# The second mixer of a two-layer trunk put as a whole into a region of fixed instruction order

## The chip, the cores and the metric

The kernel runs on one core of a Trainium2 chip. The metric is the device time of one execution in microseconds (us); lower is better. In the kernel before, three timed runs gave a median of 1370.22 us.

## The reference

512 tokens of width 1024 pass through two layers, with 16 learned tokens put in front (528 columns in all). Layer 0 is a sparse attention and layer 1 a differential attention over a shared key and value set; after each stands a gated feed-forward block with a short convolution. The part that matters here is layer 1's mixer:

```python
kv = rms_norm(h, kv_norm_g) @ w_kv_b
k1, k2, vb = jnp.split(kv, [...], axis=-1)
k1 = rms_norm(k1.reshape(B, Tp, N_HEADS, B_HEAD_DIM), kn_b)
k2 = rms_norm(k2.reshape(B, Tp, N_HEADS, B_HEAD_DIM), kn_b)
...
def attn_map(qb, kk):
    lg = jnp.einsum('bqhd,bshd->bhqs', qb, kk).astype(jnp.float32) * scale + bias
    return jax.nn.softmax(jnp.where(mask, lg, NEG_INF), axis=-1)
a = attn_map(q1b, k1) - lam * attn_map(q2b, k2)
o = jnp.einsum('bhqs,bshd->bqhd', a.astype(vb.dtype), vb)
...
o = rms_norm(o, sub_g) * (1.0 - lam_init)
return o.reshape(B, Tp, N_HEADS * B_V_DIM) @ w_o
```

## The kernel before

**Data.** The residual stream `ht` lies in SBUF as eight tiles of 128 features by 528 tokens. Every projection is float32 made of three matmuls: a weight is cast to a short float32 by ScalarE (`hi`, L168), the remainder is taken by VectorE or GpSimd (`lo`, L176), the activations are split alike (`xh`, `xl`), and TensorE (`lin`, L306) adds hi·hi, hi·lo and lo·hi. A weight's way is a DMA on SyncE (L115), a scaling by the norm's gains on GpSimd (`raw`, L123), then `hi` and `lo`; three buffers of each kind rotate, and the work for the unit three ahead is written into the source where a unit ends (`done`, which calls `pump`).

**The second mixer** (`mixer_b`, L1471) starts with the norm of the first 272 columns, still missing from `ffn(0)`, then takes four pairs of heads p = 0 to 3. `project(p)` (L1500) makes two key, two query and two value projections of 48 matmuls each. When one ends, ScalarE and VectorE take it out of PSUM: keys as squares `sq` and scaled `kg` (L1513, L1514), queries as `qst` twice and `sq` (L1529 to L1532), values as `vf` (L1571). TensorE then sums squares (`stk` L671, `stq` L681), the reciprocal roots are made on ScalarE and VectorE (`rsqrt`, L470 to L478), GpSimd spreads a key's root (`ex`, L698) and TensorE turns it (`Rk`, L703); values are turned too (`vt`, L713).

`attend_b` (L1605) runs 16 units, two heads by two halves of the queries per pair. A unit scores the next unit's blocks (`sb`, L1670 and L1671; VectorE adds the bias and takes the minimum, L1673; ScalarE takes the exponential, L1679; VectorE combines the two maps, L1689 to L1692) while it multiplies its own with the values, in steps: a transpose `pt` (L1759), `ph` by ScalarE (L1763), `pl` by VectorE (L1764), and three matmuls `pv` (L1745); at its end ScalarE copies `of` (L1767). Between the pieces `fill` (L274) takes matmuls of the projections from a generator, 6 at a time as a rule, until a model clock of the source has gone on by the gap that the pair asks for (`GAP_B`). A generator may hand back nothing: query projections of a pair wait until attention has come to a certain unit. `defer` writes a piece into the source once the model clock has passed a delay. `finish_sums` (L1780) writes the squares of the outputs (`sqo`, L1788) and, straight behind them, their sum on TensorE (`stq`); `finish_roots`, `Ro` (L1819) and `split_out` finish a pair's outputs, and `wo_first` and `wo_last` multiply them with the output weights.

```python
def sums(e):
    sq = bp.tile([128, T], F32, tag="sq", name="sqo", bufs=2)
    nc.scalar.activation(sq[:, t0:t1], of[:, e, t0:t1], AF.Square)
    st = self.query_stats(sq, self.ones, blocks)
```

**What sets the order.** The program is built with `schedule_with_timeline_sim=True`: a scheduler plays the instructions through on a model of the engines and issues, on each engine, what is ready, the earlier in the source first. `high_priority` lets the norm's pieces go ahead by 200 places. In `ffn` the 20 paired blocks stand in `tc.manual_schedule(engines=ENGINES)`, where TensorE, VectorE and ScalarE (`ENGINES`) keep the source's order; GpSimd and SyncE are always left to the scheduler. There the casts are placed by hand (`early`, `late`, with `auto = False`); in `mixer_b` they stand where `done` calls `pump`. PSUM has two tiles of two banks (tag `sp`: `lin`, `Rk`, `vt`) and four of one bank (tag `one`: `sb`, `pt`, `pv`, the sums).

Of the kernel before, what the change touches and what calls it, by code (L numbers as in the profile page):

```python
# [15 lines left out]
ENGINES = {mybir.EngineType.PE, mybir.EngineType.DVE, mybir.EngineType.Activation}  # L16
# [1860 lines left out]
@with_exitstack  # L1877
def trunk_kernel(ctx, tc, aps, out):
    t = Trunk(ctx, tc, aps, out)
    t.setup()  # L1880
    t.mixer_a()
    t.ffn(0)
    t.mixer_b()
    t.ffn(1)


# [53 lines left out]
```

## Time and profile before

| | |
|---|---|
| median of 3 runs | 1370.22 us (1365.03 to 1372.44) |
| the profiled execution | 1369.62 us, span 1367.8 us |
| TensorE matmul busy | 1284.9 us, 94% of the span |
| VectorE busy | 1032.4 us, 75% |
| ScalarE busy | 716.7 us, 52% |
| GpSimd busy | 343.3 us, 25% |
| mean granted TensorE clock | 0.975 of full speed |

Busy time of TensorE holds the time in which a matmul is under way, pipelined ones included, so the distance from start to start is shorter than a row's mean duration. An engine's "idle before" is the time before an instruction in which the engine did nothing, with the releaser that ended it. A granted clock of 1.00 is 2.4 GHz, 0.50 is 1.2 GHz, and a value between is a mean over a stretch that had both. The second mixer lies between about 655 and 985 us of the span.

### The profile page before, as it was taken

What the parts mean: (1) busy time and instruction counts of PE and PEld (TensorE: products, weight loads), DVE (VectorE), ACT (ScalarE), POOL (GpSimd) and SP (SyncE); (2) the same over time, 40 slices, a digit from 0 to 9 for tenths busy, and PEclk for the clock granted to TensorE, in tenths of its full rate; (3) what the DMA queues carried; (4) which work ended last, traced back from release to release, by engine and by line L of the source; (5) the groups of instructions that cost most, each with busy time, mean ns of one, the idle gap of its engine ahead of it and who ended that gap; (6) DMA issues with size and microseconds to landing.
All of it is one profiled execution on the core that took longest, in us unless ns stands there. A gap on an engine that the chain in (4) does not pass through costs nothing.

```text
span 1367.8 us, 25126 instructions
## 1 busy us (share of the span) xinstructions
PE 1284.9 (94%) x9688; PEld 1233.5 (90%) x9688; DVE 1032.4 (75%) x2030; ACT 716.7 (52%) x1426; POOL 343.3 (25%) x398
## 2 busy tenths in 40 slices
PE   5999889897999999989899999989897999999998
PEld 4999889897999999989799999989787999999986
DVE  6499977687888888776657777776787888888873
ACT  4453555564555555554435555655464555555541
POOL 3513543410111111103444644444510111111100
PEclk9999999989999999999899989999999999999999
DMA  7312222121455445533222222212221454554432
GB/s 236 107 61 76 88 83 80 62 78 62 117 133 146 127 125 130 132 79 106 92 63 89 68 67 63 71 48 73 67 88 62 120 146 129 127 148 127 118 90 93
DMA packets 58519, 136.03 MB, mean 99 GB/s; under 512 B 7216, under 2 KB 16736, under 8 KB 58400
## 3 DMA queue, kind: packets, MB, share of 16 engines
q1 hardware_dynamic: 48432, 114.57, 25.7%
q0 software_dynamic: 9968, 19.87, 9.5%
q8 instruction: 76, 1.25, 0.4%
q14 instruction: 43, 0.35, 0.1%
HBM read 112.46 MB, written 4.91 MB: 86 GB/s over the span
## 4 chain that ended last, share of the span: by engine, by line
PE 80%; DVE 11%; ACT 4%; issue 2%; POOL 1%; DMA 1%; SPq 0%; ACTq 0%; DVEq 0%; POOLq 0%
PE lin L306 22%; PE dn L1374 18%; PE g L1240 17%; PE v L1240 12%; DVE c L1331 2%; PE pv L1745 1%; PE stq L681 1%; PE pv L1119 1%; PE linh L306 1%; DVE lo L176 1%; DVE xl L630 1%; ACT hi L168 1%; PE sa L1024 1%; PE stk L671 1%; PE sb L1671 1%
## 5 line engine op out<-in xcount | busy, mean ns | idle before, releaser
L306 PE MATMUL lin<-xh,hi 128*128 128x256 f32 (+3 forms) x928 | 272.2, 298 | 13.6 <-DVE ht L547 7.1
L306 PE MATMUL lin<-xl,hi 128*128 128x256 f32 (+3 forms) x928 | 272.3, 295 | 2.1 <-DVE xl L630 1.8
L306 PE MATMUL lin<-xh,lo 128*128 128x256 f32 (+3 forms) x928 | 271.8, 294 | 0.0
L168 ACT CAST hi<-raw 128x512 fp32r<-128x512 f32 (+3 forms) x225 | 178.8, 824 | 90.9 <-PE lin L306 47.6
L176 DVE TENSOR_TENSOR lo<-raw,hi 128x1024 fp32r<-128x1024 f32 (+3 forms) x196 | 179.1, 929 | 55.1 <-ACT hi L168 52.1
L1410 POOL DMA_DIRECT2D ht<-y x64 | 55.8, 872 | 569.3 <-ACT y L1409 560.6
L306 PEld LDWEIGHTS lin<-xh,hi 128*128 128x128 f32 (+1 forms) x928 | 179.7, 196 | 17.1 <-ACT xh L656 8.6
L306 PEld LDWEIGHTS lin<-xl,hi 128*128 128x128 f32 (+1 forms) x928 | 181.2, 195 | 3.8 <-DVE xl L630 3.2
L306 PEld LDWEIGHTS lin<-xh,lo 128*128 128x128 f32 (+1 forms) x928 | 181.1, 195 | 0.0
L1240 PE MATMUL g<-xh,hi 128*128 128x264 f32 (+1 forms) x480 | 137.3, 286 | 11.3 <-DVE c L1331 6.6
L1374 PE MATMUL dn<-al,hi 128*128 128x256 f32 (+2 forms) x528 | 143.0, 321 | 0.0
L1374 PE MATMUL dn<-ah,lo 128*128 128x256 f32 (+2 forms) x528 | 142.2, 320 | 0.0
L1374 PE MATMUL dn<-ah,hi 128*128 128x256 f32 (+2 forms) x528 | 142.2, 321 | 0.0
L1240 PE MATMUL v<-Th,lo 128*128 128x264 f32 (+1 forms) x480 | 136.9, 285 | 0.0
L1240 PE MATMUL v<-Tl,hi 128*128 128x264 f32 (+1 forms) x480 | 136.5, 284 | 0.0
L1240 PE MATMUL v<-Th,hi 128*128 128x264 f32 (+1 forms) x480 | 136.3, 284 | 0.0
L1240 PE MATMUL g<-xh,lo 128*128 128x264 f32 (+1 forms) x480 | 136.0, 283 | 0.0
L1240 PE MATMUL g<-xl,hi 128*128 128x264 f32 (+1 forms) x480 | 135.7, 283 | 0.0
L1240 PEld LDWEIGHTS g<-xh,hi 128*128 128x128 f32 x480 | 90.4, 188 | 15.4 <-ACT hi L168 7.7
L176 DVE TENSOR_TENSOR lo<-S,hi 128x1024 fp32r<-128x1024 f32 x80 | 97.2, 1216 | 0.0
L1374 PEld LDWEIGHTS dn<-ah,lo 128*128 128x128 f32 x528 | 89.0, 188 | 7.4
L1374 PEld LDWEIGHTS dn<-ah,hi 128*128 128x128 f32 x528 | 88.8, 188 | 5.7 <-ACT hi L168 1.1
(301 smaller groups left out, 3290.7 us busy)
## 6 DMA issues: line engine op xcount, KB each, us to landing
raw<-w_up SPq DMA_DIRECT2D x88, 512.0 KB, 3.7
raw<-w_down SPq DMA_DIRECT2D x64, 256.0 KB, 3.5
ht<-y POOLq DMA_DIRECT2D x32, 264.0 KB, 3.9
raw<-w_in SPq DMA_DIRECT2D x16, 512.0 KB, 3.6
raw<-w_kv SPq DMA_DIRECT2D x16, 512.0 KB, 3.6
ht<-y POOLq DMA_DIRECT2D x32, 256.0 KB, 3.8
raw<-w_down SPq DMA_DIRECT2D x16, 384.0 KB, 3.2
nb<-nbias SPq DMA_DIRECT2D x16, 264.0 KB, 2.7
```

The costliest lines, as they stand in the source:

```text
L168: nc.scalar.copy(hi[:, :n, :m], src)
L176: eng.tensor_tensor(lt[:, :n, :m], src, hi[:, :n, :m].bitcast(F32), op=OP.subtract)
L306: i = self.nc.tensor.matmul(o, w[wi][:, kw + k, :m], x[s][xi][:, kx + k, c0:HN[s]], start=(first and p == 0), stop=(last and p == 2))
L630: i = eng.tensor_tensor(xl[:, m, o:o + n], xfs[m][:, :n], xh[:, m, o:o + n].bitcast(F32), op=OP.subtract)
L671: self.nc.tensor.matmul(st[:88, 2 * c:2 * c + 2], sq[:, 88 * c:88 * (c + 1)], rhs, start=True, stop=True)
L681: self.nc.tensor.matmul(st[:, c:c + 2], sq[:, c0:c0 + 128], rhs, start=True, stop=True)
L1024: nc.tensor.matmul(s, q[:, c0:c0 + 128], k[:, k0:k1], start=(p == 0), stop=(p == 2))
L1119: nc.tensor.matmul(pv[:, :4 * nq], v[:, c, :], pp[:, :, :nq], start=(ci == 0 and p == 0), stop=(ci == nch - 1 and p == 2))
L1240: nc.tensor.matmul(out, w[wi][:, wk + k, :], xs[xi][:, xk + k, c0:c0 + N], start=(first and k == 0 and p == 0), stop=(k == 3 and p == 2), ...
L1331: nc.vector.scalar_tensor_tensor(t[:, z:n], u[:, off + t0 + z - d:off + T - d], w, t[:, z:n], op0=OP.mult, op1=OP.add)
L1374: nc.tensor.matmul(part(t, c0, c1, o), w[wi][:, k, :], acts[f][ai][:, c0:c1], start=(first and p == 0), stop=(last and p == 2))
L1410: nc.gpsimd.dma_start(self.h[m][:, t0:T], y[:, :n], accum_op=OP.add)
```

## The change

The call of `mixer_b` is put into the region that `ffn` already uses. The statements in it and their order in the source stay as they are.

```diff
     t.setup()
     t.mixer_a()
     t.ffn(0)
-    t.mixer_b()
+    with tc.manual_schedule(engines=ENGINES):
+        t.mixer_b()
     t.ffn(1)
```

Of the orders of TensorE, VectorE and ScalarE, all rows of the second mixer may move. Three places follow; the attention of the second pair of heads runs in each of them, beside the projections of the third.

ScalarE, where `finish_sums` for the first pair is written, behind the second key projection. Before:

```order
L1679 ACTIVATE xs,ss<-xs,sm 128x272
L1679 ACTIVATE xs,sm<-xs,sm 128x272
L168 CAST hi<-raw 128x1024
L1529 ACTIVATE qst<-lin,gs 64x528
L1767 COPY of<-pv 128x272
L1788 ACTIVATE sqo<-of 128x528
L1763 CAST ph<-pt 128x256
```

With the change:

```order
L1763 CAST ph<-pt 128x256 x3
L1513 ACTIVATE sq<-lin 128x528
L1514 ACTIVATE kg<-lin,par 128x528
L168 CAST hi<-raw 128x1024
L1788 ACTIVATE sqo<-of 128x528 x2
L1763 CAST ph<-pt 128x128
```

The squares `sqo` stood by themselves between pieces of attention, and now stand behind the evacuation of a key projection and a weight cast. On TensorE, in the change, the sum `stq<-ones,sqo` follows `pt` with no matmul between.

VectorE, where the first key projection of the third pair ends. Before:

```order
L1692 SCALAR_TENSOR_TENSOR xx<-xx,sm 128x400
L1764 TENSOR_TENSOR pl<-pt,ph 128x128
L1673 ISA xs,sm<-sb,tm,rq 128x272
L1673 ISA sm 128x1
L1673 ISA xs,sm<-sb,tm,rq 128x272
L1673 ISA sm 128x1
L1689 RECIPROCAL sm<-sm 128x1
L1690 SCALAR_TENSOR_TENSOR sm<-ss,nlam,sm 128x1
L1692 SCALAR_TENSOR_TENSOR xs<-xs,sm 128x272
L176 TENSOR_TENSOR lo<-raw,hi 128x1024
```

With the change:

```order
L1692 SCALAR_TENSOR_TENSOR xx<-xx,sm 128x528
L176 TENSOR_TENSOR lo<-raw,hi 128x1024
L1689 RECIPROCAL sm<-sm 128x1
L1690 SCALAR_TENSOR_TENSOR sm<-ss,nlam,sm 128x1
L1692 SCALAR_TENSOR_TENSOR xx<-xx,sm 128x400
L1673 ISA xs,sm<-sb,tm,rq 128x272
L1673 ISA sm 128x1
L1673 ISA xs,sm<-sb,tm,rq 128x272
L1673 ISA sm 128x1
L1519 TENSOR_SCALAR rk<-stk 88x12
L1764 TENSOR_TENSOR pl<-pt,ph 128x256
```

The weight's remainder `lo` moved ahead of a combination and of two score reductions, which stand in the queue behind it now.

TensorE, where the first query projection of the third pair has ended and the generator of projections hands back nothing. Before, a piece of the same unit:

```order
L306 MATMUL lin<-xh_8145,hi 128x272
L306 MATMUL lin<-xl_8146,hi 128x272
L1745 MATMUL pv<-pl,vh 128x256
L1745 MATMUL pv<-ph,vl 128x256
L1759 MATMUL pt<-ident,xx 128x128 x2
L306 MATMUL lin<-xh_8145,lo 128x272
L306 MATMUL lin<-xh_7979,hi 128x256
L306 MATMUL lin<-xl_7980,hi 128x256
L1670 MATMUL sb<-kst,qst 128x16
L1671 MATMUL sb<-kl_8073,qst 128x16
L306 MATMUL lin<-xh_7979,lo 128x256
```

With the change, 12 rows out of a run of 25 instructions without a `lin`:

```order
L1745 MATMUL pv<-ph,vl 128x272
L1759 MATMUL pt<-ident,xs 128x128 x2
L1670 MATMUL sb<-kst,qst 128x400
L1671 MATMUL sb<-kl_8071,qst 128x400
L1670 MATMUL sb<-kst,qst 128x400
L1671 MATMUL sb<-kl_8079,qst 128x400
L681 MATMUL stq<-ind,sq 128x2 x5
L1745 MATMUL pv<-ph,vh 128x256
L1745 MATMUL pv<-pl,vh 128x256
L1745 MATMUL pv<-ph,vl 128x256
L1759 MATMUL pt<-ident,xs 128x128
L1745 MATMUL pv<-ph,vh 128x128
```

The matmuls of projections that stood between the steps of attention are gone from this piece. The order of the change has four such long runs in the second mixer: of 43, 25, 25 and 81 instructions.

## Rows read from the trace of the kernel before

**Rows 1.** Windows, 655 to 1005 us: busy us (count) of PE, PEld, DVE, ACT, POOL; PEclk, DMA share, GB/s.
```profile
730.00:972.00 242.00, 232.99 (x1864) 228.03 (x1863) 174.07 (x524) 136.37 (x359) 111.95 (x133) 0.96 0.23 69
...
sum 350.00, PE 327.65 PEld 319.49 DVE 245.78 ACT 185.86 POOL 163.62; mean PE 109.22 PEld 106.50 DVE 81.93 ACT 61.95 POOL 54.54
```

**Rows 2.** Waits of PE, 655 to 1005 us: total, times, longest.
```profile
PE lin L306 <- DVE ht L547: 6.2, 5, 2.3
PE pv L1745 <- DVE pl L1764: 3.0, 2, 1.7
PE Rk L703 <- POOL ex L698: 2.4, 2, 2.0
PE lin L306 <- ACT xh L656: 2.3, 2, 1.4
PE lin L306 <- DVE xl L630: 1.8, 2, 1.1
...
PE R L619 <- DVE nr L612: 0.6, 2, 0.4
```
**Rows 3.** Groups on ACT, 720 to 975 us: busy us, mean ns | idle before.
```profile
L168 ACT CAST hi<-raw 128x1024 fp32r<-128x1024 f32 x18 | 18.7, 1041 | 5.4 <-PE lin L306 3.6 <-issue 1.7
L1763 ACT CAST ph<-pt 128x256 fp32r<-128x256 f32 x40 | 14.2, 361 | 5.8 <-PE pt L1759 5.1 <-PE pv L1745 0.4
...
L1529 ACT ACTIVATE qst<-lin,gs 64x528 fp32r<-64x528 f32 x12 | 8.3, 694 | 4.0 <-DVE qst L1532 4.0
...
L1514 ACT ACTIVATE kg<-lin,par 128x528 f32<-128x528 f32 x6 | 4.2, 692 | 0.0
L1788 ACT ACTIVATE sqo<-of 128x528 f32<-128x528 f32 x6 | 3.8, 640 | 0.5 <-PE stk L671 0.5
...
L1513 ACT ACTIVATE sq<-lin 128x528 f32<-128x528 f32 x6 | 3.6, 602 | 0.0
L1571 ACT COPY vf<-lin 128x528 f32<-128x528 f32 x6 | 3.5, 581 | 0.0
```
**Rows 4.** Groups on DVE, the same stretch.
```profile
L176 DVE TENSOR_TENSOR lo<-raw,hi 128x1024 fp32r<-128x1024 f32 x15 | 19.4, 1291 | 6.3 <-ACT hi L168 6.3
L1764 DVE TENSOR_TENSOR pl<-pt,ph 128x256 fp32r<-128x256 f32 x40 | 16.3, 413 | 5.1 <-ACT ph L1763 4.9
L1690 DVE SCALAR_TENSOR_TENSOR sm<-ss,nlam,sm 128x1 f32<-128x1 f32 x32 | 12.9, 404 | 0.9
...
L1673 DVE CUSTOM_DVE_ANT_0 xs<-sb,tm,rq 128x272 f32<-128x272 f32 x16 | 7.8, 494 | 0.7 <-PE sb L1671 0.5
L1673 DVE DVE_READ_ACCUMULATOR2_ANT sm<- 128x1 f32 x80 | 6.5, 82 | 0.0
...
L1692 DVE SCALAR_TENSOR_TENSOR xx<-xx,sm 128x400 f32<-128x400 f32 x8 | 5.6, 699 | 0.2
...
L1689 DVE RECIPROCAL sm<-sm 128x1 f32<-128x1 f32 x32 | 5.1, 159 | 4.8 <-ACT xs L1679 3.5 <-ACT xx L1679 0.8
...
L473 DVE TENSOR_TENSOR rk<-rk 88x24 f32<-88x24 f32 x3 | 1.4, 476 | 0.1
```
**Rows 5.** Groups on POOL, the same stretch.
```profile
L698 POOL TENSOR_SCALAR ex<-rk 88x768 f32<-88x768 f32 x6 | 5.6, 932 | 6.1 <-DVE rk L476 3.5 <-PE Rk L703 2.6
```
**Rows 6.** Timeline (start, us, what): the pace of `lin`, and one place where `sq` stands behind `hi`.
```profile
675.79 0.29 PE L306 MATMUL lin<-xl,hi 128*128 128x272 f32 x1
675.91 0.28 PE L306 MATMUL lin<-xh,lo 128*128 128x272 f32 x1
676.11 1.04 ACT L168 CAST hi<-raw 128x1024 fp32r<-128x1024 f32 x1 [2.20 <-PE lin L306]
...
677.72 1.10 PE L671 MATMUL stk<-ind,sq 128*88 128x2 f32 x12 [1.28 <-ACT sq L1513]
```
**Rows 7.** Windows: two stretches of 10 and 55 us at a lower clock.
```profile
700.00:710.00 10.00, 8.03 (x48) 7.86 (x48) 7.50 (x13) 4.41 (x8) 9.04 (x7) 0.66 0.19 53
655.00:710.00 55.00, 47.44 (x335) 45.73 (x336) 33.68 (x61) 24.00 (x45) 28.03 (x41) 0.84 0.26 79
```

## The prediction

> **What bounds the kernel now.** I read the views in this order: the table of busy times, the windows over the second mixer, the waits of TensorE there, the groups of ScalarE, VectorE and GpSimd by shape, and the timeline at two places. TensorE is busy for 94% of the span, and in the stretch of the second mixer, 655 to 1005 us in three windows, for 327.65 of 350 us [rows 1]: it bounds, and it stands still for 22.35 us. The reader is to see which of these waits are of the mixer's inside. Those on `ht`, `xh`, `xl` and `R` (6.2 + 2.3 + 1.8 + 0.6 = 10.9 us, [rows 2]) belong to the norms and the output projection. The rest, 22.35 - 10.9 = 11.4 us, is what the order of the middle costs today: `pv` on `pl` 3.0, `Rk` on `ex` 2.4 [rows 2], small ones for the rest. VectorE is busy for 174.07 of the middle's 242 us and ScalarE for 136.37 [rows 1]: neither bounds over the whole stretch, but both have long pieces that others queue behind, `lo` of 1.29 us [rows 4] and `hi` of 1.04 us [rows 3]. The scheduler hides these by giving TensorE matmuls of a projection, which start 0.12 us apart at full clock (675.79 and 675.91, [rows 6]). The middle's granted clock is 0.96 [rows 1].
>
> **The change part by part.** No instruction is added or removed, and no DMA; three queues lose the right to go around what isn't ready. GpSimd and SyncE are still left to the scheduler, so weights and bias tables keep their lead (three buffers of each), and I cost them at nothing. So each term is a place where, in the written order, TensorE's own matmuls run out before a queue of ScalarE or VectorE has delivered.
>
> First, the start. The sum of squares for the first 272 columns now stands behind all 48 matmuls that covered it, so root, reciprocal and `R` are bare: the like chain waited 0.6 us twice in all [rows 2], and the strict order of the `xl` pieces adds about the same again. I take 1.5 us, between 0.6 and the 4.1 that `xh` and `xl` cost now [rows 2].
>
> Second, ends of the first key unit of pairs 1 to 3. ScalarE has to go through `ph` 0.36, `sq` 0.60, `kg` 0.69 and `hi` 1.04 = 2.7 us [rows 3]; only then can VectorE begin `lo`, 2.7 + 1.29 = 4.0, and behind it stand a combination (0.16 + 0.40 + 0.70 = 1.26) and two score reductions of 0.49 + 0.08 [rows 4]: 6.4 us. TensorE has before it some 30 instructions at 0.12, 3.7 us, until it wants a PSUM bank that these reductions free. 6.4 - 3.7 = 2.7, three times: 8.1 us.
>
> Third, the sums of the outputs. `stq` stands straight behind `sqo`, which stands behind the second key unit's end: 0.36 + 0.60 + 0.69 + 1.04 + 0.64 = 3.3 us on ScalarE [rows 3], with no `lin` for TensorE; the second head's `sqo`, 0.64 and its hop, brings 4.0. Twice so, and the last pair in its halves about 2.0: 10.0 us.
>
> Fourth, ends of the second query unit. ScalarE: 0.69 + 0.69 + 0.60 + 1.04 = 3.0 us, `lo` until 4.3; attention's `pl` stands behind that and TensorE waits about 0.9 for it. Then the roots, 0.48 and some five small operations between 0.16 and 0.40 [rows 4], at 0.3: 6.3; then `ex`, 0.93 [rows 5]: 7.2, against some 48 matmuls, 5.8 us. That is 0.9 + 1.4 + 0.4 for the second `Rk` = 2.7, three times, and 2.0 in the first pair, which has no attention beside it: 10.1 us.
>
> Fifth, the largest: the four runs of TensorE without a `lin`, of 43, 25, 25 and 81 instructions. They come where the generator of projections hands back nothing (a pair's queries wait for a unit of attention, the output weights wait for unit 12). A bare step of attention is 8 instructions or so, 1.0 us, for TensorE, and for VectorE `pl` 0.41, two reductions at 0.57 and a combination at 1.26 = 2.8 us [rows 4]: 1.8 us lost per step. The run of 43 has five steps (15 `pv`), those of 25 three each: 9.0 + 5.4 + 5.4. That of 81 has six (18 `pv`), 10.8, and two sums and the outputs' roots one after the other, about 1.2 + 1.2 + 1.8: 15.0. Together 34.8 us. Two ends: half of it, if the engines come into a run with work done ahead, and all of a serial chain `pt`, `ph`, `pl`, `pv`, some 6 us more.
>
> Sixth, value ends: `vf` 0.58 and `hi` 1.04 ahead of the next `ph` [rows 3]; most have 42 matmuls of the next unit right behind. Between 0 and 1.0 each for six; I take 0.5, 3.0 us, since most are covered.
>
> Sum: 1.5 + 8.1 + 10.0 + 10.1 + 34.8 + 3.0 = 67.5. Of today's 11.4 us I take all as gone, since these places have a price of their own in the sum. Net 56.1 us on the profiled execution's 1369.62, which lies 0.6 under the median: 1425.7, so **1426 us**.
>
> **One thing the sum holds still** is the clock. Rows first: over the first 55 us, where TensorE is idle for 7.6 us, the granted clock is 0.84, and within it 10 us with 2 us idle ran at 0.66 [rows 7], a mix of the 2.4 and 1.2 GHz levels. If the middle, with 60 us more idle, went from 0.96 to 0.84, its 233 busy us would take 233 x (0.96 / 0.84 - 1) = 33 us more: 1459. The sum without that stays my forecast because busy stretches between the new waits are as a rule many times longer than the waits. The Trainium skill ("TensorE: Matmul & The Clock Gate", section "HAM oscillation") speaks against this change: it describes a kernel in which a wait came between all bursts of matmuls, so that each burst began at half rate again. By that rule the time would be the 1459 of this paragraph, by the rows of the middle as it is 1426.
>
> **The rivals.** *The clock falls too* (about 1445 to 1470): the mechanism and price just given. For it speaks that the four long runs and the ends of units make waits of 2 to 4 us in every pair like the one of [rows 7]; against it that most of TensorE's work stays in long rows of `lin`.
>
> *The covers mostly hold.* VectorE is free for 28% of the middle [rows 1], and the written order may let it run ahead into each place. Then only the long runs cost: 34.8 - 11.4 = 23.4, 1393; with half of them 17.4 - 11.4 = 6, 1376. Against it: the unit ends put `hi` and `lo` ahead of attention in a queue that can't be passed.
>
> *Faster.* The scheduler inverts pieces at places: at 676 us `hi` goes ahead of `sq` and TensorE waits 1.28 us [rows 6]; `Rk` waits 2.0 at once [rows 2], in a stretch whose clock is 0.66 [rows 7]. A written order has `sq` ahead of `hi`. If it took these waits away (1.3 + 2.4 + 3.0, [rows 2, 6]) with the slow 10 us (10 x 0.34 = 3.4) and the queues ran dry nowhere, it would be 1369.6 - 10.1 = 1360. It decides as soon as the new waits sum to under 10 us, that is, if a bare step cost below 0.5 and a unit's end nothing. Against it: the run of 81 alone comes to 15.
>
> *The change does nothing*: excluded by the order, in which all of the three engines' rows move.
>
> **How the numbers follow.** A measurement of this kernel tells about 0.5% (7 us) from no change. Forecast (1400 to 1445) 0.50; clock (1445 to 1470) 0.20; covers hold (1377 to 1400) 0.20; faster 0.06; same 0.04. The range, 1385 to 1465, leaves out faster and same (0.10), the better half of the case of covers that hold, and the end of the clock's. So faster 0.06, same 0.04, slower 0.90.
>
> **What would show it.** Right: in the changed profile TensorE's idle time from 655 us on grows from 22 to some 75 us and its busy time hardly; `stq` waits on `sqo` for over 2.5 us in each of the two later pairs, `Rk` on `ex` in each pair, `pv` and `sb` on VectorE in the long runs, where TensorE is busy for under half of the time; the spans before 655 us and of the last feed-forward block stay. Wrong in size: unit ends without such waits (covers hold), or TensorE's busy time up by over 20 us at a middle's clock under 0.90 (clock). Wrong in sign: no wait over 2 us in the middle, and idle time below 22 us. A GpSimd or SyncE queue that comes late in the chain of waits would be a cause I have not priced.

## The result and the profile after

The changed kernel takes 1509.97 us (median of four runs, 1506.06 to 1515.35) against 1371.33 us for the kernel before (four runs): 1.102 times as long, 95% interval 1.0965 to 1.1073. The prediction was 1426 us in a range of 1385 to 1465: the sign was right, the loss of 139 us is 2.5 times the one forecast.

The head of the page of the changed kernel; the last line is the granted clock in 40 slices of the span, in tenths of full speed:

```profile
span 1508.2 us, 25105 instructions
...
PE 1355.2 (90%) x9688; PEld 1288.3 (85%) x9688; DVE 1030.8 (68%) x2030; ACT 720.2 (48%) x1426; POOL 335.5 (22%) x398
...
PEclk9999999999999999988878787787978999999999
```

The same 9688 matmuls, and TensorE is busy for 1355.2 us instead of 1284.9: 70 us more. It stands still for 153.0 us instead of 82.9: another 70 us. Both halves of the loss lie in the second mixer. The windows of the changed kernel (stages: up to the first `sb`, attention up to the last `pv`, what is behind it up to the next feed-forward block, and all three; columns as in [rows 1]):

```profile
655.00:726.40 71.40, 62.44 (x439) 59.81 (x439) 36.07 (x70) 28.45 (x53) 30.62 (x44) 0.83 0.22 70
726.40:1078.50 352.10, 284.65 (x1784) 266.39 (x1783) 177.18 (x525) 135.09 (x353) 98.67 (x131) 0.79 0.15 44
1078.50:1148.50 70.00, 53.30 (x361) 50.98 (x359) 29.45 (x71) 24.57 (x55) 26.53 (x20) 0.83 0.20 64
655.00:1148.50 493.50, 400.39 (x2578) 377.18 (x2578) 242.69 (x666) 188.10 (x460) 155.82 (x195) 0.80 0.17 51
```

And those of the kernel before, cut at the same events; its mixer, too, reaches up to the feed-forward block at 1006 us, so further than the 985 us named in the section on the time before:

```profile
655.00:724.50 69.50, 61.68 (x455) 59.79 (x456) 39.86 (x73) 29.58 (x55) 32.09 (x44) 0.88 0.26 75
724.50:966.10 241.60, 233.65 (x1868) 228.90 (x1868) 173.17 (x527) 136.03 (x357) 112.87 (x135) 0.96 0.23 69
966.10:1006.00 39.90, 33.32 (x261) 31.80 (x261) 32.75 (x68) 20.80 (x50) 18.66 (x16) 0.96 0.25 80
655.00:1006.00 351.00, 328.65 (x2580) 320.49 (x2581) 245.78 (x668) 186.40 (x462) 163.62 (x195) 0.94 0.24 71
```

The mixer went from 351.0 to 493.5 us: idle from 22.4 to 93.1 us (+70.7), busy from 328.65 to 400.39 (+71.7). The start is 2 us longer, attention 110, the tail 30. The granted clock of the whole fell from 0.94 to 0.80: of the busy time, 328.65 x 0.06 = 20 us were lost to it before, and 400.39 x 0.20 = 80 us are now. That is 60 of the 72. Taken in windows of 1 us, each one's busy time times what its clock lacks, it is 18.9 us before and 83.0 now: 64 of the 72. What the other 8 are was not settled.

What TensorE waits for in this stretch, which answers to [rows 2]:

```profile
PE sb L1670 <- DVE sm L1673: 18.5, 19, 3.6
PE stq L681 <- ACT sq L1531: 13.1, 8, 3.2
PE stq L681 <- ACT sqo L1788: 11.2, 5, 3.0
PE pv L1745 <- ACT ph L1763: 7.6, 9, 1.1
PE lin L306 <- DVE ht L547: 7.1, 2, 6.7
PE pt L1759 <- DVE xx L1692: 6.6, 5, 1.7
PE Rk L703 <- POOL ex L698: 4.9, 5, 1.4
PE lin L306 <- ACT xh L1833: 4.3, 2, 2.7
PE lin L306 <- POOL xl L1834: 3.8, 2, 2.7
PE vt L713 <- ACT vf L1571: 3.2, 4, 0.9
```

The idle time is spread over many pieces: scores that wait for a bank (`sb`), both kinds of sums (`stq`), products, transposes, and the output side (`xh`, `xl`, `ht`). The other two engines tell more. Their longest waits in the changed kernel:

```profile
DVE pl L1764 <- ACT ph L1763: 73.3, 58, 2.7
...
ACT ph L1763 <- PE pt L1759: 70.3, 32, 7.0
ACT xx L1679 <- DVE sm L1673: 37.4, 24, 2.5
```

The same waits in the kernel before:

```profile
DVE pl L1764 <- ACT ph L1763: 7.1, 11, 1.9
...
ACT ph L1763 <- PE pt L1759: 15.1, 12, 3.1
ACT xx L1679 <- DVE sm L1673: 13.7, 13, 4.6
```

VectorE waited 7.1 us for `ph` before and 73.3 us now. All three engines wait for one another in turn, while VectorE and ScalarE have as much to do as before (242.7 against 245.8 us and 188.1 against 186.4, in the windows above). The timeline of the changed kernel shows it at one place (ScalarE's rows first, then VectorE's, then TensorE's):

```profile
851.00 0.74 ACT L1679 ACTIVATE xx<-xx,sm 128x528 f32<-128x528 f32 x1 [2.39 <-DVE sm L1673]
...
851.73 0.36 ACT L1763 CAST ph<-pt 128x272 fp32r<-128x272 f32 x1
853.72 0.74 ACT L1679 ACTIVATE xx<-xx,sm 128x528 f32<-128x528 f32 x1 [1.62 <-DVE sm L1673]
...
852.13 0.44 DVE L1764 TENSOR_TENSOR pl<-pt,ph 128x272 fp32r<-128x272 f32 x1 [1.17 <-ACT ph L1763]
852.49 0.49 DVE L1673 CUSTOM_DVE_ANT_0 xx<-sb,tm,rq 128x272 f32<-128x272 f32 x1
...
853.14 0.54 DVE L1673 CUSTOM_DVE_ANT_0 xx<-sb,tm,sm 128x256 f32<-128x256 f32 x1
...
857.61 1.65 PE L681 MATMUL stq<-ind,sq 128*128 128x2 f32 x10 [3.23 <-ACT sq L1531]
```

Exponential, `ph`, `pl`, reductions, next exponential: each begins where the one before ends, and neither ScalarE nor VectorE may take anything else meanwhile. TensorE's 3.23 us before `stq` stand at the end of such a chain.

### The profile page after: what moved, and what is told of

Read it like the earlier page. It is cut to its first block, busy times and chain, and to the rows that moved or that the text cites. A ratio compares the mean times of both kernels' runs of the same rounds, so it can differ in the third digit from the quotient of the medians.

```text
span 1508.2 us, 25105 instructions
## 1 busy us (share of the span) xinstructions
PE 1355.2 (90%) x9688; PEld 1288.3 (85%) x9688; DVE 1030.8 (68%) x2030; ACT 720.2 (48%) x1426; POOL 335.5 (22%) x398
## 4 chain that ended last, share of the span: by engine, by line
PE 74%; DVE 12%; ACT 8%; issue 3%; DMA 1%; POOL 1%; SPq 0%; DVEq 0%; ACTq 0%; POOLq 0%
PE lin L306 21%; PE dn L1374 17%; PE g L1240 15%; PE v L1240 11%; DVE c L1331 2%; PE pv L1745 2%; ACT hi L168 2%; PE stq L681 2%; DVE lo L176 1%; PE pv L1119 1%; PE linh L306 1%; DVE xx L1673 1%; ACT xx L1679 1%; PE pt L1759 1%; PE sa L1024 1%
## 5 line engine op out<-in xcount | busy, mean ns | idle before, releaser
L306 PE MATMUL lin<-xh,hi 128*128 128x256 f32 (+3 forms) x928 | 294.7, 319 | 19.6 <-DVE ht L547 8.0
L306 PE MATMUL lin<-xl,hi 128*128 128x256 f32 (+3 forms) x928 | 284.2, 307 | 5.9 <-POOL xl L1834 3.8
L306 PE MATMUL lin<-xh,lo 128*128 128x256 f32 (+3 forms) x928 | 282.6, 305 | 0.0
L176 DVE TENSOR_TENSOR lo<-raw,hi 128x1024 fp32r<-128x1024 f32 (+3 forms) x196 | 178.3, 925 | 77.3 <-ACT hi L168 71.7
L306 PEld LDWEIGHTS lin<-xh,hi 128*128 128x128 f32 (+1 forms) x928 | 195.0, 211 | 23.0 <-ACT xh L656 13.0
L306 PEld LDWEIGHTS lin<-xl,hi 128*128 128x128 f32 (+1 forms) x928 | 195.0, 210 | 7.9 <-POOL xl L1834 4.2
L306 PEld LDWEIGHTS lin<-xh,lo 128*128 128x128 f32 (+1 forms) x928 | 194.2, 209 | 0.0
L1240 PE MATMUL g<-xh,hi 128*128 128x264 f32 (+1 forms) x480 | 136.9, 285 | 11.3 <-DVE c L1331 6.6
```

The source lines that it names most:

```text
L176: eng.tensor_tensor(lt[:, :n, :m], src, hi[:, :n, :m].bitcast(F32), op=OP.subtract)
L306: i = self.nc.tensor.matmul(o, w[wi][:, kw + k, :m], x[s][xi][:, kx + k, c0:HN[s]], start=(first and p == 0), stop=(last and p == 2))
L1240: nc.tensor.matmul(out, w[wi][:, wk + k, :], xs[xi][:, xk + k, c0:c0 + N], start=(first and k == 0 and p == 0), stop=(k == 3 and p == 2), ...
```

## The experiments

The theory with which the runs began (A): the written order leaves holes at TensorE, and each lowers the clock, which gives half of the loss. Theory E came with the fourth run: the three fixed queues are in step with one another, so that no single late piece makes the holes. Each experiment is one run; the kernel before, run beside each group of them, took 1368.05 to 1374.07 us, and the four runs of the changed kernel lie 9.3 us apart, so a gain of 6 us is no more than noise.

**Which queue.** The region for a part of the engines.

```diff
-    with tc.manual_schedule(engines=ENGINES):
+    with tc.manual_schedule(engines={mybir.EngineType.PE}):
```

> The order of TensorE alone is fixed in the second mixer; VectorE and ScalarE are left to the scheduler. Theory A (the written order runs TensorE dry because the queues of ScalarE and VectorE can't be passed, and each hole lowers the clock): part of the loss stays, since TensorE still has no matmuls between the pieces, but the evacuations are no longer behind the casts; about 1400 to 1450 us. Rival C (it is TensorE's own order that costs): 1490 to 1510 us. Rival D (TensorE's order costs nothing by itself): 1365 to 1380 us.

1450.4 us, at the upper end of A.

```diff
-    with tc.manual_schedule(engines=ENGINES):
+    with tc.manual_schedule(engines=ENGINES - {mybir.EngineType.PE}):
```

> The orders of VectorE and ScalarE are fixed, TensorE's is left to the scheduler. Theory A: TensorE can take other ready matmuls, but the scheduler's model decides, so some holes stay; 1385 to 1440 us. Rival C (TensorE's order costs): 1365 to 1380 us. Rival D (the queues of VectorE and ScalarE cost): 1480 to 1510 us.

1488.6 us: 121 of the 139 us with TensorE free, so A's figure was wrong and rival D's right.

```diff
-    with tc.manual_schedule(engines=ENGINES):
+    with tc.manual_schedule(engines={mybir.EngineType.Activation}):
```

> Only ScalarE's order is fixed. With the orders of VectorE and ScalarE both fixed the time was 1488.6 us. If ScalarE's queue is what makes the others late: 1450 to 1490 us. If VectorE's is: 1370 to 1400 us.

1447.8 us: fixing ScalarE alone costs 76 us over the kernel before beside it (1371.3), nearly as much as fixing TensorE alone (82 over 1368.1); the time lies 2 us under the range that stood for ScalarE. TensorE's 82 and the other two's 121 add up to far more than the whole. One queue that can't be passed is enough to hold up the two that can; VectorE alone was not tried. In these three runs TensorE's idle time grew by 44, 60 and 40 us over the page of before and its busy time by 37, 59 and 39: the two halves go together each time.

**Is it the clock that the holes cost?** First the holes ahead of the sums were filled with matmuls of no use.

```diff
+            self.dm = bp.tile([128, 256], F32R, name="dm")
+            self.nc.gpsimd.memset(self.dm.bitcast(F32), 1.0)
...
         st = self.ps.tile([128, 512], F32, tag="one", name="stq")
+        for _ in range(warm):
+            self.nc.tensor.matmul(st[:, :256], self.dm[:, :128], self.dm[:, :256], start=True, stop=True)
```

> The changed kernel with matmuls of no use (18 or 6 of 128x256 on a tile of ones) ahead of each group of sums stq, into the bank that stq then writes. They do not shorten the wait for sq or sqo, they only keep TensorE busy in it. Theory A (half of the loss is the clock, which falls behind the holes): the 24 us of holes ahead of stq are filled, the slow stretches behind them go, 1480 to 1500 us and a mean granted clock above 0.94. Rival B (the slow stretches have another cause than the holes): 1508 to 1520 us at a clock of 0.93, since the added matmuls delay what follows by a little.

1503.1 us at a mean clock of 0.948 (0.928 in the changed kernel). The time misses A's range by 3 us, the clock is in it. The mixer's window:

```profile
655.00:1141.00 486.00, 403.72 (x2784) 381.69 (x2785) 243.18 (x668) 189.23 (x462) 155.49 (x196) 0.86 0.18 52
```

With some 206 more matmuls recorded it is busy for only 3 us more, and at 0.86 the clock takes 403.72 x 0.14 = 57 us instead of 80. So filling the holes ahead of `stq` gave back some 23 us of clock, and the fillers ate most of it; the 7 us that are left of the gain are within the noise.

Then holes were put where there were none: into the last feed-forward block of the kernel before, ahead of each of 32 down projections, with one copy by ScalarE or with five.

```diff
                 t, w = new(), ws.take()
+                if l == 1:
+                    nc.tensor.matmul(t[:, :256], w[0][:, 0, :], acts[f0][0][:, :256], start=True, stop=True)
+                    for _ in range(1):
+                        nc.scalar.copy(self.pause, t[:, :256])
                 for k in range(f1 - f0):
```

> The price of a hole by itself. The kernel before, with 32 waits put into TensorE's densest stretch, the last feed-forward block, where TensorE is busy throughout at a granted clock of 1.00: ahead of each down projection one matmul of 256 columns writes the bank, ScalarE copies it once to a scratch tile, and TensorE's next matmul waits for that copy, some 0.7 us each, 22 us in all. Theory A (a hole costs its own length and about as much again by the clock): 1410 to 1420 us, with TensorE's busy time up by 15 us or more beside the 32 added matmuls (some 4 us). Rival B (holes cost their length alone): 1388 to 1400 us, clock as before. Rival H (only longer holes lower the clock): as B here, as A in the run with long holes.

> The same with five copies by ScalarE, one after the other, so some 2.2 us a hole, 70 us in all, about as much as the change added in the second mixer. Theory A: 1490 to 1520 us, TensorE's busy time up by 50 us or more. Rival B: 1435 to 1455 us, busy time as before but for the added matmuls.

1443.9 and 1534.4 us against 1374.07 of the kernel before beside them: both over every range given. The holes came out longer than meant, 1.18 and 1.96 us by turns in the short run and 2.8 and 3.6 in the long one, since the copies also wait in ScalarE's queue. What decides is TensorE's busy time and clock, not the total. The waits, of the short run first:

```profile
PE dn L1374 <- ACT pause L1408: 50.3, 32, 2.0
```

```profile
PE dn L1374 <- ACT pause L1408: 101.8, 32, 3.6
```

The windows of this block, in the kernel before, the short run and the long run:

```profile
1060.00:1315.00 255.00, 255.00 (x1770) 238.34 (x1770) 210.18 (x292) 142.26 (x225) 27.87 (x32) 1.00 0.50 129
1060.00:1385.00 325.00, 274.74 (x1749) 249.18 (x1748) 205.21 (x286) 148.63 (x254) 27.00 (x31) 0.95 0.38 100
1060.00:1478.00 418.00, 315.56 (x1806) 285.21 (x1806) 211.40 (x295) 200.01 (x386) 27.87 (x32) 0.87 0.31 79
```

On the pages TensorE's busy time grew by 25.6 us in the short run (1310.5 against 1284.9) and by 63.7 us in the long one (1348.6); the 32 added matmuls account for 8.9 us of records in each (279 ns a piece). So with no piece of the order changed, 50.3 us of holes cost 16.7 us of slower matmuls, and 101.8 us cost 54.8: a third and a half of their length. The clock, taken in windows of 1 us as above, accounts for 15.2 and 52.4 of these. Theory A's price, as much again as the hole, was too high here. Rival H, that only longer holes count, is right in part: in the short run the clock fell nine times, each time at one of the 16 holes of 1.96 us and never at one of the 16 of 1.18 us; in the long run it fell at 31 of the 32. Windows behind one hole of the long run show how:

```profile
1121.00:1122.00 1.00, 0.84 (x4) 0.70 (x5) 0.00 (x0) 0.64 (x2) 0.00 (x0) 1.00 0.00 0
1122.00:1123.00 1.00, 1.00 (x6) 0.80 (x5) 0.00 (x0) 0.00 (x0) 0.00 (x0) 0.78 0.08 16
1123.00:1124.00 1.00, 1.00 (x6) 1.00 (x6) 0.00 (x0) 0.00 (x0) 0.00 (x0) 0.50 0.00 0
...
1125.00:1126.00 1.00, 1.00 (x5) 0.90 (x5) 0.00 (x0) 0.42 (x1) 0.00 (x0) 0.51 0.00 0
1126.00:1127.00 1.00, 1.00 (x5) 0.82 (x5) 0.61 (x1) 0.87 (x2) 0.00 (x0) 1.00 0.00 0
```

TensorE comes out of the hole at 2.4 GHz, then is busy throughout at 1.2 GHz for some 3 us, and is back. Rival B falls: holes lower the clock by themselves. In the mixer a us of hole costs 1.0 us of busy time (71.7 to 70.7) and only a third to a half here. Holes that follow one another before the clock is back would explain it, though no run puts them at other distances; this window from the longest of the four stretches without a `lin` in the changed kernel is of that kind:

```profile
1004.00:1024.00 20.00, 12.55 (x46) 10.36 (x46) 8.61 (x34) 7.04 (x21) 6.11 (x9) 0.53 0.15 46
```

Twenty us, of which TensorE works 12.55, at 0.53; from 1006 to 1032 us the clock stays at 0.50 throughout.

**Is it single late pieces?** Four edits took one of them away each. First the sums, written later:

```diff
-            self.defer(1.62, lambda: stats_q(m, sq))
+            self.defer(1.62 + 3.2, lambda: stats_q(m, sq))
...
+            self.defer(self.LATE, lambda: total(e, sq))
+
+        def total(e, sq):
             st = self.query_stats(sq, self.ones, blocks)
...
+    LATE = 3.2
```

> The changed kernel with the sums on TensorE written later: stq of the queries 3.2 us of the source's clock later, stq of the outputs 3.2 us behind its sqo rather than straight behind it. Theory A: the 24 us of waits of stq go, and with them some 17 us of slow clock: 1460 to 1480 us. Rival E (what a written order takes from one wait goes to the next, since ScalarE and VectorE are late by then anyway): 1495 to 1510 us.

1504.0 us, as rival E had it. The waits of `stq` are gone from the list, and others stand in their place:

```profile
PE pv L1745 <- ACT ph L1763: 26.2, 14, 6.2
PE sb L1670 <- DVE sm L1673: 21.6, 19, 3.4
```

Next the query's square, written ahead of the copies:

```diff
+            nc.scalar.activation(sq, src, AF.Square)
             for e in range(2):
...
-                if e == 1:
-                    nc.scalar.activation(sq, src, AF.Square)
```

> The changed kernel with the query's square sq written ahead of the two copies qst rather than behind the first. The 13 us in which stq waits for sq should go for the most part. Theory A (each hole is one late piece, and the clock gives as much again): 1480 to 1492 us. Rival E (the queues of ScalarE and VectorE are late as a whole, so that the wait goes to the next piece, as when the sums were written later): 1500 to 1512 us.

1511.5 us, nothing. `stq` no longer waits for `sq`, but `pv` for `ph` 10.4 us instead of 7.6, `Rk` for `ex` 9.0 instead of 4.9, and `pt` for `sm` 6.7 instead of 0.7:

```profile
PE pv L1744 <- ACT ph L1762: 10.4, 12, 2.2
...
PE pt L1758 <- DVE sm L1672: 6.7, 2, 3.4
```

The casts at the ends of units, which stand in four of the prediction's six terms:

```diff
+        def late():
+            self.defer(2.0, self.wt.done)
...
-            yield from self.lin(x, lambda u, m=m: evac_q(u, m))
+            yield from self.lin(x, lambda u, m=m: (evac_q(u, m), late()), done=False)
```

The key and value units got the same edit.

> The changed kernel with the work of a unit's end on the next weights (hi, lo, load and scaling) written 2 us of the source's clock later, so that hi and lo no longer stand straight behind the evacuation and ahead of ph, pl and the reductions. Theory F (the casts at the ends of units make the holes, as the prediction had it): 1460 to 1485 us. Rival E (they only stand ahead of other pieces a little later): 1500 to 1515 us.

1503.9 us: theory F, the prediction's own for the ends of units, falls too, for a delay of 2 us. Last, the loop of the timeline above was cut, by writing a step's exponentials behind its `ph`.

```diff
-                nc.scalar.activation(xx[:nq, :K], xx[:nq, :K], AF.Exp, bias=sm[:nq, w + 1:w + 2], scale=-1.0,
-                                     accum_out=dst)
+                exps.append(lambda xx=xx, w=w, dst=dst: nc.scalar.activation(
+                    xx[:nq, :K], xx[:nq, :K], AF.Exp, bias=sm[:nq, w + 1:w + 2], scale=-1.0, accum_out=dst))
...
                     nc.scalar.copy(ph[:, q0:n], pt[:, q0:n])
+                    flush_exps()
```

> The changed kernel with the exponentials of a step written behind that step's ph on ScalarE rather than ahead of it. In the trace of the changed kernel a bare step is a chain with no slack: reductions, then the exponential, then ph, then pl, then the next step's reductions, 2.4 to 3.1 us a step. Theory G (this loop between the fixed queues of ScalarE and VectorE sets the pace of attention, so that VectorE waits 72 us for ph): the loop is cut, ph goes as soon as pt is there, VectorE's wait for ph falls below 40 us, and the time to 1400 to 1460 us. Rival E (the queues are late as a whole, the wait goes elsewhere): 1490 to 1515 us.

1488.2 us, the largest gain of one edit, 22 us; it lies between the ranges of theory G and rival E. VectorE waits less for `ph`, but ScalarE now waits for `pt`:

```profile
DVE pl L1770 <- ACT ph L1768: 46.9, 46, 2.7
...
ACT ph L1768 <- PE pt L1764: 122.2, 57, 7.0
```

The loop is a part of it, about a sixth of the loss, not the cause of the whole.

**Do the stages pay for themselves?** The region around the attention alone.

```diff
-            self.fill(self.LEAD_B)
-            self.next_x = [None, None]
-            self.attend_b()
+            with tc.manual_schedule(engines=ENGINES):
+                self.fill(self.LEAD_B)
+                self.next_x = [None, None]
+                self.attend_b()
```

> The region of fixed order holds only the attention and the projections beside it (from the first fill to the end of attend_b); the norm, the first pair's projections and everything behind attention are left to the scheduler as before. In the changed kernel the stretch behind the last pv is 70 us long against 40 before, and the start 2 us longer. Theory A (each stretch pays for its own holes): the tail's 30 us come back, 1475 to 1485 us. Rival (the tail is long because attention hands its work over late): 1495 to 1510 us.

1480.9 us, as theory A had it. Its windows, by the same stages:

```profile
655.00:718.40 63.40, 55.05 (x437) 53.43 (x437) 36.26 (x68) 27.18 (x49) 32.33 (x44) 0.95 0.23 74
718.40:1070.50 352.10, 285.18 (x1789) 267.45 (x1789) 176.00 (x527) 136.02 (x355) 100.03 (x132) 0.79 0.14 44
1070.50:1118.90 48.40, 45.22 (x355) 44.05 (x355) 31.34 (x70) 23.42 (x52) 24.52 (x20) 0.93 0.29 93
```

Attention takes 352.1 us as in the changed kernel; the start is 8 us shorter and the tail 21.6. So the total came out as forecast for a reason that holds in part: the tail gave back 21.6 of its 30 us, and the start more than the 2 that it had lost. The same with the last edit, and with three edits at once:

> The same edit with the region of fixed order around the attention alone, which by itself gave 1480.9 us. Theory G and stretches that pay for themselves: the gain of the edit plus 27 us, 1375 to 1435 us. Rival E: 1465 to 1485 us.

1468.0 us, in rival E's range.

> The region around the attention alone, with the exponentials behind ph, the query's squares first and the casts late, all at once. Alone against the changed kernel's 1510: region -27, exponentials -20, squares 0, casts -6. If what each takes away is free of the others: 1455 to 1465 us. If several late pieces hide one another and go together: 1400 to 1450 us.

1456.7 us: within the noise of single runs the gains add up and the pieces do not hide one another; this is 24 us under the region around the attention alone, and nowhere near the 110 us that attention has lost. And the edit with everything scheduled, as in the kernel before:

> The kernel before, all scheduled, with the same edit. If the scheduler already lets ph go ahead of the exponentials: 1362 to 1380 us, no difference that counts. If the edit helps whatever sets the order: under 1362 us.

1367.5 us against 1368.8 beside it: no difference. The two traces show why: by the names of their tiles, all 9688 matmuls, 2030 pieces of VectorE and 1418 of ScalarE come in the same sequence, so the scheduler had found this order already. No version tried beats the kernel before by more than noise.

## Why the prediction was right in sign and wrong in size

| step of the prediction | forecast | measured |
|---|---|---|
| first, the start | 1.5 us | idle +1.1 (8.96 against 7.82) |
| second and fifth, key ends and long runs | 42.9 | `sb` 18.5, `pv` 10.6, `pt` 7.3: 36.4 |
| third, sums of the outputs | 10.0 | 11.2 |
| fourth, query ends | 10.1 | `stq` on `sq` 13.1, `Rk` 4.9: 18.0 |
| sixth, value ends | 3.0 | 3.2 |
| the output side | 0 | tail's idle +10.1 |
| net idle | 56.1 | 70.7 |
| the clock | 0 | busy +71.7 |

**The step that failed** is "One thing the sum holds still is the clock". Its reason was that "busy stretches between the new waits are as a rule many times longer than the waits"; but the ten rows of waits shown count 61 of them in 493 us, one in 8 us, of 1.3 us each (80.3 in all). Nor would the reason have been enough: in the run with short holes TensorE works 274.7 us between 50.3 us of holes, over five times as long, and its clock still falls from 1.00 to 0.95. The kernel's own rows gave the warning: 0.66 over the 10 us with 2 us idle [rows 7]. The paragraph went on to price the fall, at 33 us, and that was small as well: it set 0.84, the clock of a stretch with 14% idle, for the middle, and the mixer came out with 19% idle at 0.80, the attention at 0.79. The sum and that rival's price together, 56 + 33, would have said 1459; the time is 51 us above it: 15 from the idle side and 39 from TensorE's busy time (31 of it the clock, 8 not settled), with some 2 given back outside the mixer. The prediction had named the sign of this itself: busy time up by over 20 us at a middle's clock under 0.90. It came as +71.7 and 0.79.

The Trainium skill ("TensorE: Matmul & The Clock Gate", section "HAM oscillation") had it the right way: in the kernel that it describes, waits of DMA between all bursts of matmuls bring the slow clock back each time. The run with long holes agrees in that the clock fell at 31 of 32 holes; it differs in that the burst shown began at full rate (1.00 in the window of 1121) and fell behind its first microsecond.

**Near in the idle time, wrong in its mechanism.** The idle time came out within 15 us, and part of that is luck, since two errors stand against each other. The four long runs without a `lin` hold 26.1 us of idle time (5.5, 4.8, 4.5 and 11.3) against the 34.8 of the fifth term; and TensorE is not busy for under half of the time in them but for 59 to 67%, at a clock of 0.59 to 0.77. The rest of the mixer holds 67.0 us, where the prediction's other terms and the 10.9 us of norms and outputs come to 43.6. The waits of `stq` on `sqo` came as said (3.0, 3.0 and 2.5 us). But the prediction held that single pieces (`hi`, `lo`, `sqo`) stand in the way, each with its price. Moving three pieces (the sums, `sq`, the casts) away one at a time gave 0 to 6 us, and cutting the loop 22. The lists of waits after each edit fit a wait that was one link of a chain through all three queues, so that its time went to the next link; most of attention's 110 us no edit took away, and what would is open. Two places were not priced: `stq` behind `sq` at the ends of query units, where the two engines alternate on `qst` (ScalarE waits for VectorE between its two copies), and the output side, where `ht` stands behind the next norm's pieces in VectorE's queue (6.7 us at once).

**The rivals.** "The covers mostly hold" and "faster" fell by the first window. "The clock falls too" was the right one, at 0.20, with a price less than half of what it took. Nothing of GpSimd or SyncE came late in a way that the prediction left open, but `xl` of the outputs on GpSimd (3.8 us).

## What to carry to other kernels

Price a hole at TensorE with its clock: here a microsecond of waiting cost another third to half when the holes were some 10 us apart, and a whole one in this mixer, where they came closer together in places. Before fixing an order on several engines at once, look for the loops in the written order that go through two engines and back, and count on their sum, not on the longest piece; here the one loop that was cut gave back a sixth of the loss. In this kernel the order of the source was not the one that the scheduler had issued; whether fixing the order that it did issue would keep the time was not tried.

## What the runs showed of the hardware

At 789 us of the changed kernel a piece of VectorE was slow beside one of GpSimd:

```profile
789.36 3.05 DVE L1563 TENSOR_TENSOR kl<-kg,kst 64x528 fp32r<-64x528 f32 x1 [0.70 <-ACT kst L1560]
...
794.89 1.75 DVE L1563 TENSOR_TENSOR kl<-kg,kst 64x528 fp32r<-64x528 f32 x2 [0.70 <-ACT kst L1560]
```

One `kl` took 3.05 us; two of the same shape took 1.75 us five microseconds later. In the long one GpSimd was scaling a weight:

```profile
789.95 1.89 POOL L123 TENSOR_TENSOR raw<-raw,par 128x1024 f32<-128x1024 f32 x1
```

Of the 32 `kl` in the two kernels, four lay beside such a scaling for over 1 us and took 1.72 to 3.05 us; the other 28, most of them beside other pieces of GpSimd, took 0.69 to 1.22. No run here set the two apart, and what it costs the kernel was not measured.
